# Output projections by seven quarter products: the last branch's additions and the sums of merged quarters on the vector engine, half of the sums ahead of the last branch tiles

## The chip, the core and the metric

The kernel runs on one core of a Trainium2 chip. The core has engines that run their own instruction rows side by side and wait for each other by semaphores. The profile calls them PE (TensorE, matrix products), PEld (its weight loads), DVE (VectorE), ACT (ScalarE), POOL (GpSimd) and SP (SyncE, which issues most of the loads). The metric is the device time of one execution in microseconds (us). Matrix products read their operands from the on-chip memory SBUF and write into banks of a second memory, PSUM; POOL's instructions in this kernel work on SBUF alone.

## What is computed

Two layers of a hybrid encoder on 512 tokens of width 1024. Each layer runs three branches (a pooling mixer, a sparse attention, an attention into memory tokens). What this change touches is the end of a layer, where the branches are projected, weighted by gates, added up and projected once more:

```python
for l in range(DEPTH):
    ...
    g = jax.nn.sigmoid(gates).reshape(b, s, N_BRANCH, D_MODEL)
    merged = (g[:, :, 0] * (y_pool @ w_branch[l, 0])
              + g[:, :, 1] * (y_attn @ w_branch[l, 1])
              + g[:, :, 2] * (y_mem @ w_branch[l, 2]))
    x = x + merged @ w_out[l]
return rms_norm(x, final_g)
```

## The kernel before

**Numbers in two parts.** Every float32 operand of a matrix product is split into a rounded high part and the rest (hi and lo), and a product is three matmuls: hi with hi, hi with lo, lo with hi. For a weight chunk of 128x1024, ACT writes the high part (`whi`, L172) and DVE the low part (`wlo`, L151 or L176, raw minus high). For activations `split_scaled` does the same with a factor: ACT writes the high part (L158), DVE the low part (L159). The normalised input of a layer stands as eight such pairs `h_hi[k]`, `h_lo[k]` (in the profile hh and hl).

**Branch tiles.** The merged sum has 1024 channels, in eight tiles j = 0 to 7 of 128 channels by 512 tokens. For each branch, a gate tile (`gate_tile`, 24 matmuls that read all eight pairs h, then a tanh on ACT) makes the gate `sg`, and a branch tile (`branch_tile`, L764) makes two tiles j from one weight chunk: 12 matmuls each into a PSUM bank, then on DVE gate plus one times bank (L771), then an addition into the tile's accumulator `acc[j]` (L775, on POOL). The branches run in the order 0, 2, 1; branch 1, the attention, is the last. After each pair of its tiles, `merge` (L781) splits the finished accumulators into the pairs `quarter` (in the profile mgh and mgl): for tiles 0 to 3 the first 256 tokens, for tiles 4 to 7 both halves of the tokens.

**Seven quarter products.** The output projection is a product of two matrices cut into quarters (first and second 256 tokens, first and second 512 channels of the sum, first and second 512 columns). Instead of eight quarter products it makes seven, from sums and differences of quarters, in Winograd's way. On the side of the activations these are four sums s1 to s4 (tiles `ms`), made by `quarter_sums(c)` (L790) in two halves: c = 0 needs the accumulators 0, 1, 4 and 5, c = 1 needs 2, 3, 6 and 7. For each c there are eight instructions of 128x256, four on DVE (L796, L797) and four on POOL (L798, L799). `quarter_split(n)` (L801) splits a sum into the pairs h, which no gate tile needs any more once the last one has read them: the sums of c = 0 go into h[0], h[2], h[4], h[6], those of c = 1 into h[1], h[3], h[5], h[7]. On the side of the weights POOL makes four differences of 128x1024 for each half c: b12 minus b11 in the place of b11 (L1000), b22 minus that (L1001, t2), b22 minus b12 in the place of b12 (L1018), b21 minus t2 in the place of b21 (L1014). L1000 overwrites b11, so it waits until DVE has read it for `wlo`; L1014 waits for b21's in the same way.

**The order of the products** (L998 to L1030): quarter by b11 into the banks `at`, quarter by b21 into two `pj` banks (24 matmuls each, first the 12 of c = 0, then the 12 of c = 1), then the second sum by t2 into `at`, the first sum by the new b11 into `tr`, and so on. In layer 0 the residual stream is then normalised for layer 1; in layer 1 the output is scaled and stored.

**What sets the order.** Each engine takes its instructions strictly in the order of its row. The rows come from the order of the code and from a scheduler that may pull an instruction ahead of others on its engine; so the place of an instruction is read from the rows of the built program. Tiles share buffers, and an instruction that writes one waits until the last reader of the tile before is done.

Of the kernel before, what the change touches and what calls it, by code (L numbers as in the profile page):

```python
# [52 lines left out]
def kernel(  # L53
# [19 lines left out]
    V, A, G, T = nc.vector, nc.scalar, nc.gpsimd, nc.tensor  # L73
# [28 lines left out]
    def s2(base, dt=F32, shape=(P, S)):  # L102
        return work.tile(list(shape), dt, tag="s2", name=nm(base), bufs=N_S2)
# [53 lines left out]
    def split_scaled(hi, lo, src, scale):  # L157
        on_act[:] = [A.mul(hi, src, scale)]  # L158
        return V.scalar_tensor_tensor(lo, src, scale, hi.bitcast(F32), op0=ALU.mult, op1=ALU.subtract)  # L159

    def chunk(src, n=1024, eng=None):
        return split_chunk(raw_chunk(src, n), n, eng)
# [27 lines left out]
    def project(c, r_hi, r_lo, nk=KT, off=0, m=P, c0=0, n=S, out=None):  # L190

        hi, lo = c
        ps = pj() if out is None else out
        for k in range(nk):
            a = slice(off + k * m, off + k * m + m)
            mm3(ps[:m, :n], hi[:, a], lo[:, a], r_hi[k][:, c0:c0 + n], r_lo[k][:, c0:c0 + n],
                k == 0, k == nk - 1)
        return ps
# [82 lines left out]
    def product(banks, a_parts, w_parts, start, by_tile=False):  # L281

        def unit(c, t):
            (a_hi, a_lo), (hi, lo) = a_parts[c], w_parts[c]
            for a in range(2):
                w = slice(a * 512, a * 512 + 512)
                tk = slice(a * 256 + t * P, a * 256 + t * P + P)
                for n, (u, v) in enumerate(((a_hi, hi), (a_hi, lo), (a_lo, hi))):
                    matmul(banks[t], u[:, tk], v[:, w], start=start and c == 0 and a == 0 and n == 0,
                           stop=c == 1 and a == 1 and n == 2, skip_group_check=True)  # L290

        order = [(c, t) for t in range(2) for c in range(2)] if by_tile else [(c, t) for c in range(2)
                                                                              for t in range(2)]
        for c, t in order:
            unit(c, t)

    def out_add(x, i, f, banks):

        for t in range(2):
            V.tensor_add(x[2 * i + t][f], x[2 * i + t][f], banks[t])  # L300
# [46 lines left out]
    for i in range(4):  # L347
# [4 lines left out]
        for a in range(2):  # L352
            if i == 0:
                c = slice(a * 512, (a + 1) * 512)
# [8 lines left out]
        for a in range(2):  # L363
            c = slice(a * 512, (a + 1) * 512)
# [42 lines left out]
    for k in range(KT):  # L407
        hi, lo = parts_k[k // 2]
        for h in range(4):
            o = banks[h // 2][:, h % 2 * M:h % 2 * M + M]  # L410
            c = slice(k % 2 * 512 + h * P, k % 2 * 512 + h * P + P)
# [94 lines left out]
    for l in range(DEPTH):  # L506
# [36 lines left out]
        for i in range(4):  # L543
            c = first_iq if l == 0 and i == 0 else chunk(w_tiled[l, TILE_AT["iq"] + i])
# [211 lines left out]
        acc, gate = {}, {}  # L756

        def gate_tile(bi, j):
            ps = tiled(l, f"g{bi}", j)
            s = s2("sg")  # L760
            A.activation(s, ps, AF.Tanh, scale=0.5)
            gate[bi, j] = s

        def branch_tile(bi, jp):  # L764
            b = "pam"[bi]
            c = chunk(w_br[l, bi, jp])
            for a in range(2):
                j = 2 * jp + a
                s = gate.pop((bi, j))
                ps = project(c, [yh[b, i] for i in range(4)], [yl[b, i] for i in range(4)], nk=4, off=a * 512)  # L770
                last = V.scalar_tensor_tensor(s, s, 1.0, ps, op0=ALU.add, op1=ALU.mult)  # L771
                if j not in acc:
                    acc[j] = s
                else:
                    G.tensor_add(acc[j], acc[j], s)  # L775
            return last

        quarter, sums = {}, {}
        first, second = slice(0, 256), slice(256, 512)

        def merge(j):  # L781
            n, c, a = j // 4, j % 4 // 2, j % 2
            for i in range(2 if n else 1):
                if a == 0:
                    quarter[i, n, c] = s2("mgh", F32R), s2("mgl", F32R)
                hi, lo = quarter[i, n, c]
                o = slice(a * 256, a * 256 + 256)
                split_scaled(hi[:, o], lo[:, o], acc[j][:, second if i else first], 0.5)

        def quarter_sums(c):  # L790
            s1, s2_, s3, s4 = (s2("ms") for _ in range(4))
            sums[1, c], sums[2, c], sums[3, c], sums[4, c] = s1, s2_, s3, s4
            for a in range(2):
                k = 2 * c + a
                o = slice(a * 256, a * 256 + 256)
                V.tensor_add(s1[:, o], acc[k][:, second], acc[4 + k][:, second])  # L796
                V.tensor_sub(s2_[:, o], s1[:, o], acc[k][:, first])  # L797
                G.tensor_sub(s3[:, o], acc[k][:, first], acc[k][:, second])  # L798
                G.tensor_sub(s4[:, o], acc[4 + k][:, first], s2_[:, o])  # L799

        def quarter_split(n):  # L801
            out = []
# [6 lines left out]
        def branch_units(bi):  # L809
            out = []  # L810
            for jp in range(4):
                out += [lambda j=2 * jp + a: gate_tile(bi, j) for a in range(2)]
                out.append(lambda jp=jp: branch_tile(bi, jp))
            return out
# [148 lines left out]
        for jp in range(4):  # L963
            for a in range(2):
                gate_tile(1, 2 * jp + a)
            branch_tile(1, jp)
            for a in range(2):
                merge(2 * jp + a)


        src = x_tok if l == 0 else x1
# [31 lines left out]
        w = w_split(b21)  # L1003
        out_add(x, 0, 0, at)
        product(pw2, [quarter[0, 1, c] for c in range(2)], w, True)
        for c in range(2):
            quarter_sums(c)
        out_add(x, 0, 0, pw2)
        out_done(l, x, 0, 0, ssq, grow if last else None)
        a_parts, w = quarter_split(2), w_split(t2)  # L1010
# [127 lines left out]
```

## Time and profile before

| | before |
|---|---|
| median of 3 runs | 1074.49 us (1073.6 to 1074.76) |
| the profiled execution, its own time | 1073.67 us |
| its span, first to last instruction | 1071.9 us |
| mean granted clock of TensorE | 0.984 of full speed |
| chain of work that ended last, by engine | PE 89%, POOL 4%, DVE 3%, issue, ACT and DMA 1% each |
| output projection of layer 0 begins | 483.4 us |
| output projection of layer 1 begins | 1010.65 us |

A row of a timeline gives the start in us from the span's start, the duration in us, the engine, the line of the kernel, the operation, the tiles it writes and reads, the shapes, how many equal instructions it stands for (x2: two, one behind the other), and in brackets the idle time just before and what ended it. A row of the waits gives who waited for whom, the sum in us, how many times, and the longest. The profile gives a start as the time at which the engine takes up an instruction; where it is held up by something other than a semaphore, that time is part of its duration.

### The profile page before, as it was taken

Reading aid. Unit: us, or ns where it says so; the run is one execution under the profiler, and the core shown is the slowest. Engines: PE = TensorE matmul, PEld = TensorE weight load, DVE = VectorE, ACT = ScalarE, POOL = GpSimd, SP = SyncE. Lnnn points to the kernel's source line nnn. Section 1 sums busy time; section 2 is a strip of 40 time slices with the busy share of each in tenths; the row PEclk is TensorE's granted clock in tenths of the full one; section 3 lists DMA queues with packets and bytes.
Section 4 is the critical chain, followed back from the end, with each engine's and each line's share of the span. In section 5 each row is a group of like instructions: output and inputs, shape, how many; then the busy total and the mean of one; then the engine's idle time right before and its main releaser. Section 6 shows DMA issues by size and latency. Waiting matters only on the chain.

```text
span 1071.9 us, 13685 instructions
## 1 busy us (share of the span) xinstructions
PE 1045.2 (98%) x4982; PEld 876.8 (82%) x4982; DVE 751.1 (70%) x1338; ACT 494.5 (46%) x900; POOL 264.3 (25%) x322
## 2 busy tenths in 40 slices
PE   9999999999999999996999999999999999999967
PEld 9888888888888888884898888888888888888845
DVE  7768878777888746355854687887768886543496
ACT  7755554322656434333564555542235554333254
POOL 3102420011242310257050042100113431011851
PEclk9999999999999999997999999999999999999969
DMA  9322234232323234230454121222332223322302
GB/s 344 127 91 89 80 111 145 79 122 102 111 72 108 97 118 156 97 121 1 169 177 133 64 105 63 79 79 94 114 108 99 98 79 106 132 97 99 118 0 79
DMA packets 37411, 114.24 MB, mean 107 GB/s; under 512 B 4184, under 2 KB 6232, under 8 KB 37344
## 3 DMA queue, kind: packets, MB, share of 16 engines
q1 hardware_dynamic: 35472, 110.20, 29.9%
q10 hardware_dynamic: 1872, 3.17, 0.8%
q8 instruction: 39, 0.64, 0.2%
q14 instruction: 28, 0.23, 0.1%
HBM read 109.14 MB, written 6.84 MB: 108 GB/s over the span
## 4 chain that ended last, share of the span: by engine, by line
PE 89%; POOL 4%; DVE 3%; issue 1%; ACT 1%; DMA 1%; SPq 0%; POOLq 0%; ACTq 0%; DVEq 0%
PE pj L86 67%; PE at L86 11%; PE pv L86 5%; PE tr L86 3%; PE tr L634 2%; POOL wraw L1000 1%; POOL wraw L1018 1%; POOL sg L775 1%; DVE mgl L159 1%; DMA x<-x 0%; POOL ow L1001 0%; DVE ms L797 0%; DVE ms L796 0%; POOL ow L1014 0%; DVE wlo L176 0%
## 5 line engine op out<-in xcount | busy, mean ns | idle before, releaser
L172 ACT CAST whi<-wraw 128x1024 fp32r<-128x1024 f32 x168 | 175.5, 1046 | 336.3 <-PE pj L86 192.5
L86 PE MATMUL pj<-hh,whi 128*128 128x512 f32 (+1 forms) x848 | 330.6, 390 | 0.0
L86 PE MATMUL pj<-hl,whi 128*128 128x512 f32 (+1 forms) x848 | 328.9, 388 | 0.0
L86 PE MATMUL pj<-hh,wlo 128*128 128x512 f32 (+1 forms) x848 | 328.8, 388 | 0.0
L151 DVE TENSOR_TENSOR wlo<-wraw,whi 128x1024 fp32r<-128x1024 f32 x140 | 179.2, 1281 | 126.8 <-ACT whi L172 126.3
L86 PEld LDWEIGHTS pj<-hh,wlo 128*128 128x128 f32 x848 | 159.3, 188 | 32.0
L86 PEld LDWEIGHTS pj<-hh,whi 128*128 128x128 f32 x848 | 159.4, 188 | 30.5
L86 PEld LDWEIGHTS pj<-hl,whi 128*128 128x128 f32 x848 | 159.4, 188 | 30.4
L775 POOL TENSOR_TENSOR sg<-sg,sg 128x512 f32<-128x512 f32 x32 | 52.3, 1636 | 230.2 <-DVE sg L771 228.2
L86 PE MATMUL pj<-yh,whi 128*128 128x512 f32 x192 | 75.2, 392 | 0.0
L86 PE MATMUL pj<-yl,whi 128*128 128x512 f32 x192 | 74.8, 390 | 0.0
L86 PE MATMUL pj<-yh,wlo 128*128 128x512 f32 x192 | 74.8, 390 | 0.0
L845 POOL TENSOR_TENSOR p<-rel,mask 128x128 f32<-128x128 f32 x16 | 7.5, 466 | 254.2 <-DMA rel<-bias_row 251.0
L845 POOL TENSOR_TENSOR p<-rel,acc 128x256 f32<-128x256 f32 (+2 forms) x48 | 61.1, 1294 | 0.5
L771 DVE SCALAR_TENSOR_TENSOR sg<-sg,pj 128x512 f32<-128x512 f32 x48 | 32.9, 685 | 35.6 <-PE pj L86 35.5
L159 DVE SCALAR_TENSOR_TENSOR mgl<-sg,mgh 128x256 fp32r<-128x256 f32 x24 | 21.8, 936 | 44.6 <-ACT mgh L158 44.6
L607 DVE MATCH_REPLACE8 acc<-m,acc 128x256 f32<-128x256 f32 (+2 forms) x96 | 51.4, 542 | 0.0
L861 DVE CUSTOM_DVE_ANT_0 p<-at,p 128x128 f32<-128x128 f32 (+1 forms) x64 | 30.0, 490 | 27.3 <-PE at L86 26.9
L606 DVE MAX8 m<-acc 128x8 f32<-128x256 f32 (+2 forms) x96 | 49.0, 548 | 0.1
L86 PEld LDWEIGHTS pj<-yh,wlo 128*128 128x128 f32 x192 | 36.1, 188 | 7.5
L86 PEld LDWEIGHTS pj<-yl,whi 128*128 128x128 f32 x192 | 36.1, 188 | 7.2
L86 PEld LDWEIGHTS pj<-yh,whi 128*128 128x128 f32 x192 | 36.1, 188 | 7.2
(258 smaller groups left out, 1867.5 us busy)
## 6 DMA issues: line engine op xcount, KB each, us to landing
wraw<-in_w_tiled SPq DMA_DIRECT2D x112, 512.0 KB, 3.3
wraw<-in_w_br SPq DMA_DIRECT2D x24, 512.0 KB, 3.5
wraw<-in_w_mv SPq DMA_DIRECT2D x8, 512.0 KB, 5.3
wraw<-in_w_av SPq DMA_DIRECT2D x8, 512.0 KB, 3.5
rel<-bias_row SPq DMA_DIRECT2D x16, 256.0 KB, 3.7
ow<-in_w_out SPq DMA_DIRECT2D x8, 512.0 KB, 3.5
wraw<-in_w_out SPq DMA_DIRECT2D x8, 512.0 KB, 3.5
wraw<-in_w_mk SPq DMA_DIRECT2D x7, 512.0 KB, 4.5
```

What stands on the lines that cost most here:

```text
L86: on_pe[:] = [T.matmul(*a, **kw)]
L151: eng.tensor_sub(out_lo, src, hi)
L159: return V.scalar_tensor_tensor(lo, src, scale, hi.bitcast(F32), op0=ALU.mult, op1=ALU.subtract)
L172: A.copy(hi[:, :n], raw[:, :n])
L606: V.max(m8, a[:, :n])
L607: V.match_replace(out=a[:, :n], in_to_replace=m8, in_values=a[:, :n], imm_value=TAKEN)
L634: T.transpose(pt[:, i * P:(i + 1) * P], col_of(qb, kb), ident)
L771: last = V.scalar_tensor_tensor(s, s, 1.0, ps, op0=ALU.add, op1=ALU.mult)
L775: G.tensor_add(acc[j], acc[j], s)
L845: G.tensor_add(probs[h][:, Q_COL[qb]:Q_COL[qb] + n], rels[h][:, 512 - n:512], mb[:, :n])
L861: V.tensor_tensor_reduce(out=pq, in0=ps[:, :n], in1=pq, op0=ALU.add, op1=ALU.min, scale=-1.0, scalar=3e38, accum_out=st[:, 0, qb:qb + 1])
L1000: G.tensor_sub(b11[c], b12[c], b11[c])
```

## The change

Three edits, in both layers:

- the additions of the last branch (branch 1) into the accumulators, eight for each layer, run on DVE; those of branch 2 stay on POOL;
- the sums s3 and s4, which were on POOL, run on DVE with s1 and s2;
- the first half of the sums (c = 0) is made behind the third pair of branch tiles (tiles 4 and 5), ahead of the last pair; the second half (c = 1) behind the last pair. Before, both stood in the code behind the second product.

```diff
@@ branch_tile
                 if j not in acc:
                     acc[j] = s
                 else:
-                    G.tensor_add(acc[j], acc[j], s)
+                    (V if bi == 1 else G).tensor_add(acc[j], acc[j], s)
@@ quarter_sums
                 V.tensor_add(s1[:, o], acc[k][:, second], acc[4 + k][:, second])
                 V.tensor_sub(s2_[:, o], s1[:, o], acc[k][:, first])
-                G.tensor_sub(s3[:, o], acc[k][:, first], acc[k][:, second])
-                G.tensor_sub(s4[:, o], acc[4 + k][:, first], s2_[:, o])
+                V.tensor_sub(s3[:, o], acc[k][:, first], acc[k][:, second])
+                V.tensor_sub(s4[:, o], acc[4 + k][:, first], s2_[:, o])
@@ the loop over the last branch's tiles
             branch_tile(1, jp)
             for a in range(2):
                 merge(2 * jp + a)
+            if jp > 1:
+                quarter_sums(jp - 2)
@@ behind the second product
         product(pw2, [quarter[0, 1, c] for c in range(2)], w, True)
-        for c in range(2):
-            quarter_sums(c)
         out_add(x, 0, 0, pw2)
```

(In the code of the change L1000 and L1001 have become L1002 and L1003; the other lines that are named here keep their numbers.)

What that makes of the rows is seen in three places, all in layer 0; in layer 1 the rows there are in the same order.

**DVE, from b11's first low part to the merge of tile 6.** sg_4414 and sg_4426 are the gates of tile 6 before and in the change; the `wlo` from `wraw` are the two halves of b11, the `wlo` from `ow` the first half of b21. Before, from the L771 of tile 5:

```order
L771 SCALAR_TENSOR_TENSOR sg_4333<-sg_4333,pj_4356 128x512
L176 TENSOR_TENSOR wlo_4539<-wraw_4514,whi_4538 128x1024
L159 SCALAR_TENSOR_TENSOR mgl_4372<-sg_2393,mgh_4371 128x256
L159 SCALAR_TENSOR_TENSOR mgl_4376<-sg_2393,mgh_4375 128x256
L176 TENSOR_TENSOR wlo_4543<-wraw_4516,whi_4542 128x1024
L176 TENSOR_TENSOR wlo_4575<-ow_4518,whi_4574 128x1024
L771 SCALAR_TENSOR_TENSOR sg_4414<-sg_4414,pj_4455 128x512
L159 SCALAR_TENSOR_TENSOR mgl_4486<-sg_2487,mgh_4485 128x256
```

In the change, from b11's first low part:

```order
L176 TENSOR_TENSOR wlo_4563<-wraw_4538,whi_4562 128x1024
L799 TENSOR_TENSOR ms_4386<-sg_2393,ms_4384 128x256
L176 TENSOR_TENSOR wlo_4567<-wraw_4540,whi_4566 128x1024
L159 SCALAR_TENSOR_TENSOR hl_159<-ms_4383,hh_151 128x512
L159 SCALAR_TENSOR_TENSOR hl_161<-ms_4384,hh_153 128x512
L159 SCALAR_TENSOR_TENSOR hl_163<-ms_4385,hh_155 128x512
L159 SCALAR_TENSOR_TENSOR hl_165<-ms_4386,hh_157 128x512
L176 TENSOR_TENSOR wlo_4599<-ow_4542,whi_4598 128x1024
L771 SCALAR_TENSOR_TENSOR sg_4426<-sg_4426,pj_4467 128x512
L775 TENSOR_TENSOR sg_2487<-sg_2487,sg_4426 128x512
L159 SCALAR_TENSOR_TENSOR mgl_4498<-sg_2487,mgh_4497 128x256
```

The low parts of four sums (hl of h[0], h[2], h[4], h[6]) now stand ahead of b21's low part and of tile 6's L771; the two low parts of b11 stand behind the merge of tile 5 and seven of the eight sums of c = 0, where before the first of them stood ahead of that merge.

**DVE, from the L771 of tile 7 to the addition of the first product to x.** sg_4447 and sg_4459 are the gates of tile 7; wlo_4579 and wlo_4603 are the low part of b21's second half. Before:

```order
L771 SCALAR_TENSOR_TENSOR sg_4447<-sg_4447,pj_4470 128x512
L176 TENSOR_TENSOR wlo_4579<-ow_4520,whi_4578 128x1024
L159 SCALAR_TENSOR_TENSOR mgl_4486<-sg_2520,mgh_4485 128x256
L159 SCALAR_TENSOR_TENSOR mgl_4490<-sg_2520,mgh_4489 128x256
L176 TENSOR_TENSOR wlo_4645<-ow_4530,whi_4644 128x1024
L300 TENSOR_TENSOR x_4497<-x_4497,at_4532 128x512
```

In the change:

```order
L771 SCALAR_TENSOR_TENSOR sg_4459<-sg_4459,pj_4482 128x512
L797 TENSOR_TENSOR ms_4510<-ms_4509,sg_2229 128x256
L775 TENSOR_TENSOR sg_2520<-sg_2520,sg_4459 128x512
L798 TENSOR_TENSOR ms_4511<-sg_2229 128x256
L799 TENSOR_TENSOR ms_4512<-sg_2487,ms_4510 128x256
L159 SCALAR_TENSOR_TENSOR mgl_4498<-sg_2520,mgh_4497 128x256
L159 SCALAR_TENSOR_TENSOR mgl_4502<-sg_2520,mgh_4501 128x256
L796 TENSOR_TENSOR ms_4509<-sg_2262,sg_2520 128x256
L798 TENSOR_TENSOR ms_4511<-sg_2262 128x256
L797 TENSOR_TENSOR ms_4510<-ms_4509,sg_2262 128x256
L176 TENSOR_TENSOR wlo_4603<-ow_4544,whi_4602 128x1024
L799 TENSOR_TENSOR ms_4512<-sg_2487,ms_4510 128x256
```

The low part of b21's second half stood directly behind the L771 of tile 7; now the merge of tile 7 and six sums of c = 1 stand between.

**POOL, at the weight differences.** Before (the L775 are the additions of tiles 4 to 7):

```order
L775 TENSOR_TENSOR sg_2360<-sg_2360,sg_4300 128x512
L775 TENSOR_TENSOR sg_2393<-sg_2393,sg_4333 128x512
L1000 TENSOR_TENSOR wraw_4514<-wraw_4522,wraw_4514 128x1024
L1001 TENSOR_TENSOR ow_4530<-ow_4526,wraw_4514 128x1024
L1018 TENSOR_TENSOR wraw_4522<-ow_4526,wraw_4522 128x1024
L1000 TENSOR_TENSOR wraw_4516<-wraw_4524,wraw_4516 128x1024
L1001 TENSOR_TENSOR ow_4531<-ow_4528,wraw_4516 128x1024
L1018 TENSOR_TENSOR wraw_4524<-ow_4528,wraw_4524 128x1024
L1014 TENSOR_TENSOR ow_4518<-ow_4518,ow_4530 128x1024
L775 TENSOR_TENSOR sg_2487<-sg_2487,sg_4414 128x512
L775 TENSOR_TENSOR sg_2520<-sg_2520,sg_4447 128x512
L1014 TENSOR_TENSOR ow_4520<-ow_4520,ow_4531 128x1024
```

In the change:

```order
L1002 TENSOR_TENSOR wraw_4538<-wraw_4546,wraw_4538 128x1024
L1003 TENSOR_TENSOR ow_4554<-ow_4550,wraw_4538 128x1024
L1018 TENSOR_TENSOR wraw_4546<-ow_4550,wraw_4546 128x1024
L1002 TENSOR_TENSOR wraw_4540<-wraw_4548,wraw_4540 128x1024
L1003 TENSOR_TENSOR ow_4555<-ow_4552,wraw_4540 128x1024
L1018 TENSOR_TENSOR wraw_4548<-ow_4552,wraw_4548 128x1024
L1014 TENSOR_TENSOR ow_4542<-ow_4542,ow_4554 128x1024
L1014 TENSOR_TENSOR ow_4544<-ow_4544,ow_4555 128x1024
```

The eight differences are now all that POOL has here. Each L1002 waits for the low part of its half of b11 on DVE, each L1014 for that of its half of b21.

On ACT the high parts of the four early sums (L158, hh of h[0], h[2], h[4], h[6]) stand ahead of the cast of b21's first half and of the last gate's tanh. The loads of the residual stream x (eight on SP) use other buffers than before, and seven of them wait for DVE's additions, sums or merges of tiles 4 and 5, or for the first of those hl.

## Prediction

> **What bounds the kernel now.** I read the page first, then the granted clock in stretches, the waits of the bad stretch, and last the timelines of the four engines there.
>
> ```profile
> PE 1045.2 (98%) x4982; PEld 876.8 (82%) x4982; DVE 751.1 (70%) x1338; ACT 494.5 (46%) x900; POOL 264.3 (25%) x322
> 455.00:491.50 36.50, 36.50 (x163) 30.08 (x161) 15.59 (x13) 8.92 (x15) 22.42 (x10) 1.00 0.27 95
> 491.50:511.20 19.70, 11.03 (x24) 6.50 (x24) 17.98 (x23) 10.59 (x19) 11.63 (x10) 0.65 0.03 11
> 511.20:530.00 18.80, 18.80 (x84) 15.54 (x83) 16.73 (x21) 9.68 (x13) 0.23 (x2) 1.00 0.46 158
> 1018.80:1040.20 21.40, 12.35 (x27) 7.67 (x27) 19.72 (x24) 10.52 (x19) 14.50 (x12) 0.60 0.00 0
> ```
>
> The columns of a stretch are its length, busy time of PE, PEld, DVE, ACT and POOL, the clock, and DMA. TensorE is the bound except in one stretch of each layer, at the start of the output projection: there PE works 11 of 19.7 us, at clock 0.65. What that costs is counted from one row of the chain of waits, where PE runs unhindered, and from PE's timeline:
>
> ```profile
> 170.87 97.71 PE pj L86 x431
> ...
> 491.34 0.39 PE L86 MATMUL pj<-whi,mgl 128*128 128x512 f32 x1
> 511.14 0.39 PE L86 MATMUL at<-wlo,hh 128*128 128x512 f32 x1
> ...
> 1018.59 0.39 PE L86 MATMUL pj<-whi,mgl 128*128 128x512 f32 x1
> 1040.23 0.39 PE L86 MATMUL at<-whi,hh 128*128 128x512 f32 x1
> ```
>
> At full clock matmuls start every 0.227 us (431 in 97.71). Layer 0: the row of 511.14 is 23 matmuls behind the first, 5.2 us, but comes 19.8 us later: 14.6 us lost. Layer 1: 27 matmuls, 6.1 us, and 21.6 us: 15.5 lost. Together 30 us; the change cannot bring more here. What PE waits for:
>
> ```profile
> ACT mgh L158 <- POOL sg L775: 14.1, 2, 11.7
> DVE mgl L159 <- ACT mgh L158: 11.6, 2, 10.0
> ACT hh L158 <- DVE ms L796: 5.2, 2, 4.4
> POOL ms L799 <- DVE ms L797: 3.4, 1, 3.4
> PE at L86 <- ACT hh L158: 2.9, 1, 2.9
> PE at L86 <- DVE hl L159: 2.6, 1, 2.6
> ```
>
> The last two merges wait for POOL's addition, and the sums come late behind them. Why POOL is late:
>
> ```profile
> 470.77 2.39 POOL L1000 TENSOR_TENSOR wraw<-wraw,wraw 128x1024 f32<-128x1024 f32 x1
> ...
> 475.66 2.57 POOL L1018 TENSOR_TENSOR wraw<-ow,wraw 128x1024 f32<-128x1024 f32 x1
> 479.39 3.31 POOL L1000 TENSOR_TENSOR wraw<-wraw,wraw 128x1024 f32<-128x1024 f32 x1 [1.16 <-DVE wlo L176]
> 482.78 2.39 POOL L1001 TENSOR_TENSOR ow<-ow,wraw 128x1024 f32<-128x1024 f32 x1
> 485.13 2.40 POOL L1018 TENSOR_TENSOR wraw<-ow,wraw 128x1024 f32<-128x1024 f32 x1
> 487.48 2.40 POOL L1014 TENSOR_TENSOR ow<-ow,ow 128x1024 f32<-128x1024 f32 x1
> 489.84 1.29 POOL L775 TENSOR_TENSOR sg<-sg,sg 128x512 f32<-128x512 f32 x1
> 493.04 2.19 POOL L775 TENSOR_TENSOR sg<-sg,sg 128x512 f32<-128x512 f32 x1 [1.92 <-DVE sg L771]
> ```
>
> Tile 6 was ready for its addition at 481.6 (the L771 below), but POOL had four weight subtractions of 2.4 us ahead of it. That queue goes with the change. The question is what takes its place.
>
> **How DVE and POOL meet.** DVE's rows in the same place:
>
> ```profile
> 468.44 1.22 DVE L176 TENSOR_TENSOR wlo<-wraw,whi 128x1024 fp32r<-128x1024 f32 x1
> L159 DVE SCALAR_TENSOR_TENSOR mgl<-sg,mgh x2: 2153/2381/2609, 471.3 to 473.4; 128x256 fp32r<-128x256 f32 x2
> 475.90 3.41 DVE L176 TENSOR_TENSOR wlo<-wraw,whi 128x1024 fp32r<-128x1024 f32 x1
> 479.24 1.21 DVE L176 TENSOR_TENSOR wlo<-ow,whi 128x1024 fp32r<-128x1024 f32 x1
> 480.88 0.69 DVE L771 SCALAR_TENSOR_TENSOR sg<-sg,pj 128x512 f32<-128x512 f32 x1 [0.44 <-PE pj L86]
> 491.61 0.76 DVE L159 SCALAR_TENSOR_TENSOR mgl<-sg,mgh 128x256 fp32r<-128x256 f32 x2 [10.04 <-ACT mgh L158]
> 502.83 1.82 DVE L796 TENSOR_TENSOR ms<-sg,sg 128x256 f32<-128x256 f32 x2
> 504.58 1.81 DVE L797 TENSOR_TENSOR ms<-ms,sg 128x256 f32<-128x256 f32 x2
> ```
>
> Two mgl take 0.76 us alone, but 2.15 and 2.61 us each beside POOL's subtractions. The wlo of 475.90 ends at 479.31, 1.1 us after the L1018 ended at 478.23; the L1000 of 479.39 ends 2.3 us after the wlo of 479.24 did. L771, whose second input is in PSUM, is not touched (0.69 beside that L1000). So a DVE instruction with two SBUF inputs and a POOL one run one after the other, and where both have work they take turns, one each: at 502.8 four sums of 0.33 us take 3.6 us beside four of POOL's. One turn is 2.3 us for a POOL subtraction; for DVE 1.13 (128x1024), 0.6 (128x512), 0.33 (128x256), from rows that follow each other.
>
> **The change part by part.** Durations are of the profiled execution: 1073.67 us, a span of 1071.9 and 1.8 around it; the median of the runs is 1074.49, 0.8 more.
>
> Additions of tiles 0 to 5 onto DVE: six of 128x512 for each layer. Their form is not in DVE's rows; the nearest are L771 (0.69) and hl (0.69 at 519.65), the contended end is 0.6 plus one turn. I take 0.6. For the first four nothing of POOL's runs beside them and DVE waits for its next cast anyway, so they cost nothing; without that cover 0.6 each.
>
> ```profile
> 462.70 1.22 DVE L151 TENSOR_TENSOR wlo<-wraw,whi 128x1024 fp32r<-128x1024 f32 x1 [4.21 <-ACT whi L172]
> 464.56 0.69 DVE L771 SCALAR_TENSOR_TENSOR sg<-sg,pj 128x512 f32<-128x512 f32 x1 [0.64 <-PE pj L86]
> ...
> 519.65 0.69 DVE L159 SCALAR_TENSOR_TENSOR hl<-ms,hh 128x512 fp32r<-128x512 f32 x1
> L796 DVE TENSOR_TENSOR ms<-sg,sg x8: 410/678/950, 501.5 to 1032.1; 128x256 f32<-128x256 f32 x8
> ```
>
> Tiles 4 and 5 with the first four sums, layer 0, from the L771 of 464.56: two L771 and two additions (2.5 with the wait between the first pair), a wait of 0.48 for ACT's mgh (as from POOL's end at 491.13 to the mgl of 491.61), four mgl (1.35), seven of the eight sums (0.33 each, 410 ns with its end: 2.3), and the wlo of the first weight half of b11 (1.13): it ends near 472.4, where before it ended at 469.66. It releases POOL's first subtraction, so POOL begins 2 us later than now (470.77), at 472.8 behind the eighth sum.
>
> From there POOL has six subtractions in a row with nothing between (no addition stops it now), and DVE has six pieces: wlo of b11's second half, the four hl that the early sums allow, and wlo of b21's first half. Taking turns they are plainly added: 6 x 2.3 + 1.13 + 4 x 0.6 + 1.13 = 18.5 us, so that wlo lands at 491.3, where before it was there at 480.45. PE wants it with the second matmul of its product, at 489.1 (the row of 491.34 is the product's twelfth): **a new wait of 2.2 us**. The product's second bank waits for the L771 of tile 6, which comes 0.6 later and is hidden behind its first six matmuls. ACT's four hh ahead of its casts cost nothing: it sat idle 3.9 us at 477.9 for the same last gate tile (the row is below).
>
> The L771 of tile 6, due at 480.88, stands behind that wlo: 491.9. Beside it POOL takes its seventh piece, L1014, to 493.7; then the addition (0.6), the wait for mgh and two mgl (1.2), four sums, L771 and addition of tile 7, two mgl and three more sums (4.2 us in all), and wlo of b21's second half (1.13): 500.9. POOL's eighth piece waits for that wlo, so it is idle meanwhile. PE wants it at 491.8, with the fourteenth matmul. **PE is then 9.1 us late in all**, the 2.2 included. Its clock is down again and comes back as now:
>
> ```profile
> 507.57 0.79 PE L86 MATMUL at<-whi,hl 128*128 128x512 f32 x1 [2.59 <-DVE hl L159]
> 510.73 0.58 PE L86 MATMUL at<-whi,hh 128*128 128x512 f32 x1
> ...
> 477.94 1.05 ACT L172 CAST whi<-ow 128x1024 fp32r<-128x1024 f32 x1 [3.90 <-PE pj L86]
> ```
>
> For 3.5 us from the restart at 507.57 matmuls start every 0.43 us (the row of 510.73 is the seventh behind it, and the first took 0.6); that is 8 of them, 1.6 us more than at full clock. So the stretch loses 10.8 us instead of 14.6 in layer 0, and instead of 15.5 in layer 1, whose rows of DVE and POOL are the same up to here. The late sums (L796 to L799 behind both products, 5 us on the chain now) are gone from the chain: the second four lie in the 500.9. What is late next is wlo of t2, at 505.4 and 506.5 behind two additions to x, POOL's last subtraction and one hl; PE asks for the first about 505.2 and the second at 507.9, so at most 0.2 us. The loads of x, which now wait for DVE's sums in SP's queue, are issued by 480, the last behind the first hl, and read at 501: free.
>
> Sum: 3.8 + 4.7 = **8.4 us off**, 1073.67 to 1065.3; on the scale of the median 1066.1. I say 1066.0. If the clock needs as long again to come back, each layer loses 1.5 more (1069); a POOL turn of 2.25 or 2.35 moves it by 0.7.
>
> **The rivals.** *DVE is not held up*: all of the 30 us come back, 1044. For it: DVE is idle 10 us at 491.61 now. Against it: 2.15 and 2.61 us for a piece of 0.33. The Trainium skill, SBUF — State Buffer, section Who interferes with whom, says that of a VectorE instruction with two SBUF inputs and a GpSimd one that reads SBUF the second to issue blocks until the first is done; by that rule this rival falls, and the trace agrees (2.61 us).
>
> *DVE goes first whenever it is ready*: POOL gets only DVE's gaps, five turns ahead of the last wlo instead of seven (4.6 us), and DVE's waits for mgh (1.2) lie beside them: 5.8 us sooner; but the remaining subtractions then fall on the hl and wlo of the next product and give back some 3.5. A net 2.3 for each layer: 1061. For it: wlo at 479.24 started ahead of L1000. Against it: that one waited for the wlo before it; after mgl, L1018 went first.
>
> *Slower: a turn costs the contended duration.* If each of the seven POOL turns takes the 3.31 us of the L1000 row and not 2.3, wlo of b21's second half comes 7.1 us later: 1065.3 + 14.1 = 1079. It decides from 0.6 us for each turn, where both gains are used up. Against it: that 3.31 holds 1.0 us of waiting for DVE, which I count on DVE's side. The Trainium skill, Perfetto Trace Analysis, section Optimizing Scalar/DVE Operations, says of GPSIMD and DVE that offloading between those two might not help, because they share a read port; by that rule the sum would be near nothing, 1074, between my forecast and this rival.
>
> *The change does its work but the new row of DVE eats it*: the 0.6 us a turn just named, 1072 to 1076.
>
> **How the numbers follow.** Turns as counted 0.71 (1062 to 1069); DVE first 0.12; not held up 0.06; used up 0.05; slower 0.06. The range 1059 to 1070 holds the first and most of the second. A measurement of this kernel can tell 0.2%, 2.1 us, from no change: faster 0.89, same 0.05, slower 0.06.
>
> **What would show it.** On PE in layer 0: a wait of about 2 us for wlo near 489, a long one for wlo near 492 to 501, none for POOL's addition and none for hh; clock below 0.8 in that stretch, 11 us lost. On DVE: the four hl from 478 to 488, each about 2.9 us, in turn with POOL; L771 of tile 6 near 491. PE without a gap from 483 to 530 would show the first rival, POOL rows of 3.3 us one after the other with a restart behind 504 the third.

## The result, and the profile after

The kernel with the change takes 1065.15 us (median of 4 runs, 1064.73 to 1066.0) beside 1074.05 us for the one before (4 runs on the same chip, 1073.39 to 1074.76): a ratio of 0.9918, with a 95% interval of 0.9901 to 0.9935. The execution that was profiled took 1064.73 us, with a span of 1062.9; before it was 1073.67 and 1071.9.

The page's first part:

```profile
PE 1038.3 (98%) x4982; PEld 873.3 (82%) x4982; DVE 773.1 (73%) x1370; ACT 494.5 (47%) x900; POOL 226.3 (21%) x290
```

Two stretches, one of each layer (length, busy time of PE, PEld, DVE, ACT and POOL, clock, DMA):

```profile
488.90:507.50 18.60, 10.90 (x39) 8.09 (x40) 18.08 (x27) 8.55 (x15) 5.03 (x3) 0.82 0.04 15
1010.00:1034.00 24.00, 16.22 (x57) 12.13 (x56) 23.48 (x28) 10.78 (x19) 10.24 (x5) 0.79 0.00 0
```

POOL is busy 38 us less and DVE 22 us more. TensorE still has one bad stretch in each layer, and beside it DVE is now busy nearly all the time (18.08 of 18.60 us), where before it was 18.0 of 19.7. What the stretch costs now, from PE's timeline (the rows of 504.72 and 1028.77 are the 27th matmul behind the first one of their layer):

```profile
488.24 0.39 PE L86 MATMUL pj<-whi,mgh 128*128 128x512 f32 x1
490.26 0.50 PE L86 MATMUL pj<-wlo,mgh 128*128 128x512 f32 x1 [1.63 <-DVE wlo L176]
...
494.99 0.50 PE L86 MATMUL pj<-whi,mgh 128*128 128x512 f32 x1 [1.93 <-ACT whi L172]
499.89 0.80 PE L86 MATMUL pj<-wlo,mgh 128*128 128x512 f32 x1 [4.41 <-DVE wlo L176]
...
502.62 0.44 PE L86 MATMUL pj<-wlo,mgh 128*128 128x512 f32 x1
...
504.72 0.40 PE L86 MATMUL at<-whi,hh 128*128 128x512 f32 x1
1011.25 0.39 PE L86 MATMUL pj<-whi,mgh 128*128 128x512 f32 x1
...
1022.94 0.79 PE L86 MATMUL pj<-wlo,mgh 128*128 128x512 f32 x1 [4.17 <-DVE wlo L176]
...
1028.23 0.47 PE L86 MATMUL at<-wlo,hh 128*128 128x512 f32 x1
...
1028.77 0.40 PE L86 MATMUL at<-whi,hh 128*128 128x512 f32 x1
```

And what PE waits for in the whole execution (us in total, times, longest):

```profile
PE pj L86 <- DVE wlo L176: 11.9, 4, 4.4
PE pj L86 <- ACT whi L172: 3.9, 2, 1.9
```

27 matmuls at full pace are 6.1 us. Layer 0: 504.72 less 488.24 is 16.5, so 10.4 us are lost. Layer 1: 17.5, so 11.4 lost. Together 21.7 where it was 30.1: 8.4 us of the 8.9 between the two profiled executions. The rest lies ahead of the stretch: the L771 of tile 4 starts at 463.96 here and at 464.56 before. In the other kernels below it starts anywhere from 463.91 (sums_only) to 465.68 (late_sums_weights), so nothing is read into it, nor into differences of about 1 us between the start times of two kernels.

DVE's timeline of layer 0 there:

```profile
463.96 0.69 DVE L771 SCALAR_TENSOR_TENSOR sg<-sg,pj 128x512 f32<-128x512 f32 x1 [0.59 <-PE pj L86]
473.03 2.63 DVE L176 TENSOR_TENSOR wlo<-wraw,whi 128x1024 fp32r<-128x1024 f32 x1 [0.72 <-ACT whi L172]
475.58 11.30 DVE L159 SCALAR_TENSOR_TENSOR hl<-ms,hh 128x512 fp32r<-128x512 f32 x4
486.81 3.40 DVE L176 TENSOR_TENSOR wlo<-ow,whi 128x1024 fp32r<-128x1024 f32 x1
490.13 0.68 DVE L771 SCALAR_TENSOR_TENSOR sg<-sg,pj 128x512 f32<-128x512 f32 x1
490.84 2.40 DVE L775 TENSOR_TENSOR sg<-sg,sg 128x512 f32<-128x512 f32 x1
498.62 1.22 DVE L176 TENSOR_TENSOR wlo<-ow,whi 128x1024 fp32r<-128x1024 f32 x1
```

And POOL's:

```profile
472.11 2.47 POOL L1002 TENSOR_TENSOR wraw<-wraw,wraw 128x1024 f32<-128x1024 f32 x1 [75.74 <-DMA x<-in_x_tok]
474.65 3.27 POOL L1003 TENSOR_TENSOR ow<-ow,wraw 128x1024 f32<-128x1024 f32 x1
477.87 2.86 POOL L1018 TENSOR_TENSOR wraw<-ow,wraw 128x1024 f32<-128x1024 f32 x1
480.69 2.84 POOL L1002 TENSOR_TENSOR wraw<-wraw,wraw 128x1024 f32<-128x1024 f32 x1
```

These rows show the turns. Four hl of 0.6 us take 11.3, because between each two of them one of POOL's subtractions runs, (11.3 - 4 x 0.6) / 4 = 2.2 us a turn; the wlo behind them takes 3.4 where it takes 1.22 alone. That wlo ends at 490.2, PE wanted it at 488.5.

### The profile page after: what moved, and what is told of

Its sections match the earlier page's. It is cut to its first block, busy times and chain, and to the rows that moved or that the text cites. A ratio compares the mean times of both kernels' runs of the same rounds, so it can differ in the third digit from the quotient of the medians.

```text
span 1062.9 us, 13690 instructions
## 1 busy us (share of the span) xinstructions
PE 1038.3 (98%) x4982; PEld 873.3 (82%) x4982; DVE 773.1 (73%) x1370; ACT 494.5 (47%) x900; POOL 226.3 (21%) x290
## 4 chain that ended last, share of the span: by engine, by line
PE 93%; DVE 5%; ACT 1%; issue 1%; POOL 0%; POOLq 0%; ACTq 0%
PE pj L86 71%; PE at L86 10%; PE pv L86 5%; PE tr L86 3%; PE tr L634 2%; DVE hl L159 2%; DVE wlo L176 1%; DVE sg L775 1%; ACT whi L172 0%; PE tr L324 0%; DVE mgl L159 0%; PE at L324 0%; DVE sg L771 0%; DVE o L333 0%; DVE ms L797 0%
## 5 line engine op out<-in xcount | busy, mean ns | idle before, releaser
L771 DVE SCALAR_TENSOR_TENSOR sg<-sg,pj 128x512 f32<-128x512 f32 x48 | 32.9, 684 | 36.0 <-PE pj L86 36.0
L775 POOL TENSOR_TENSOR sg<-sg,sg 128x512 f32<-128x512 f32 x16 | 24.6, 1536 | 100.3 <-DVE sg L771 100.3
L1002 POOL TENSOR_TENSOR wraw<-wraw,wraw 128x1024 f32<-128x1024 f32 x4 | 10.6, 2655 | 151.5 <-DMA x<-x 75.8
```

The lines of the kernel that those rows point to most:

```text
L775: (V if bi == 1 else G).tensor_add(acc[j], acc[j], s)
```

## The experiments

The theory: with the additions gone from POOL, its weight subtractions meet DVE's row directly, and the 21.7 us still lost are POOL's turns. The rivals: the early sums are what pays; DVE's own row is full; each meeting costs a fixed extra. The same numbers for all runs, each beside the kernel before on the same chip ("lost" is summed from PE's timeline of the profiled execution: each start to start in the stretch less 0.227 us). In before_weights the profiled execution took 1058.36 us, 3.2 more than the median; in the others it lies within 1.3 of it.

```
kernel               median us   ratio to before, 95%     lost, layers 0 and 1
the change           1065.15     0.9918 [0.9901, 0.9935]  10.4  11.4
adds_only            1067.38     0.9934 [0.9920, 0.9947]  11.2  12.1
late_sums            1066.79     0.9925 [0.9913, 0.9938]  10.6  12.3
sums_only            1070.17     0.9964 [0.9951, 0.9976]  13.3  13.2
weights_dve          1045.42     0.9730 [0.9717, 0.9743]  0.0   0.5
before_weights       1055.16     0.9828 [0.9815, 0.9842]  8.4   6.0
late_sums_weights    1052.07     0.9790 [0.9772, 0.9807]  2.3   5.0
pool_halves          1062.49     0.9893 [0.9879, 0.9906]  9.8   9.7
hl_held              1060.89     0.9879 [0.9865, 0.9892]  7.9   9.4
early_diffs_dve      1060.01     0.9869 [0.9856, 0.9883]  6.9   8.2
late_diffs_dve       1060.10     0.9859 [0.9840, 0.9878]  6.5   9.0
```

### The parts of the change

**adds_only**: in the change, the sums as before.

```diff
-            if jp > 1:
-                quarter_sums(jp - 2)
...
+        for c in range(2):
+            quarter_sums(c)
...
-                V.tensor_sub(s3[:, o], acc[k][:, first], acc[k][:, second])
-                V.tensor_sub(s4[:, o], acc[4 + k][:, first], s2_[:, o])
+                G.tensor_sub(s3[:, o], acc[k][:, first], acc[k][:, second])
+                G.tensor_sub(s4[:, o], acc[4 + k][:, first], s2_[:, o])
```

> Only the first edit: the last branch's additions on DVE, all sums back at their old place (half of them on POOL). Theory (turns, one each, 2.3 us for each POOL subtraction): POOL's run of subtractions starts about 471 and nothing of POOL's stands before tile 6 any more; without the four early hl fewer DVE pieces stand in the turns, so wlo of b21 lands before PE wants it, but the late sums are back behind both products, beside POOL. Counted as in the prediction, 11.6 and 12.5 us lost in the two layers against 10.9 each with the whole change: 1067, so three quarters of the gain (1074 to 1067) come from the additions alone. Rival (the sums made early are what pays): the late sums cost as before, 4 to 5 us a layer of the old loss, and this kernel stands at 1070 to 1073.

**late_sums**: the first two pieces of that diff alone, so all sums on DVE, at their old place.

> Additions and all sums on DVE, but none of the sums early. Theory: DVE does the eight sums in 0.33 us each instead of taking turns with POOL's four, some 0.3 to 1 us less for each layer than with the additions alone: 1066.5, that is, within a measurement of the whole change (1065.2): the early place of half the sums is worth at most 1 to 2 us, because it takes four hl into the turns ahead of wlo. Rival (early sums pay): 1069 or more.

**sums_only**:

```diff
-                    (V if bi == 1 else G).tensor_add(acc[j], acc[j], s)
+                    G.tensor_add(acc[j], acc[j], s)
```

> Sums as in the change, the last branch's additions on POOL as before. Theory: tiles 6 and 7 are added on POOL behind seven subtractions and hl in turns: 13.5 us lost for each layer, 1070, so the sums alone bring less than half. Rival (the additions are not what matters): within 1 us of the whole change, 1065 to 1066.

Measured: 1067.4, 1066.8 and 1070.2, each within 0.4 us of what the turns gave. PE's waits in adds_only:

```profile
PE at L86 <- ACT hh L158: 11.4, 2, 6.1
PE pj L86 <- DVE wlo L176: 0.4, 2, 0.2
```

In sums_only, one of PE's waits and one of ACT's (that one of the stretch of layer 0):

```profile
PE pj L86 <- ACT whi L172: 12.0, 2, 6.0
ACT mgh L158 <- POOL sg L775: 24.0, 4, 16.5
```

Without the early sums PE gets wlo in time and waits for the hh of the late sums instead; with the additions on POOL it waits behind POOL's addition (6.0 us for whi, whose cast stands behind mgh, and then 4.9 for wlo). So the additions bring the larger part. What the early half adds to that, 1.6 us by the medians and 0.8 by the ratios (0.9925 and 0.9918), lies inside the intervals: it takes the late sums off the chain and puts four hl, with a turn each, ahead of wlo.

### POOL's weight differences

**weights_dve**: the change, and L1002, L1003, L1014 and L1018 on DVE.

```diff
-            G.tensor_sub(b11[c], b12[c], b11[c])
-            G.tensor_sub(t2[c], b22[c], b11[c])
+            V.tensor_sub(b11[c], b12[c], b11[c])
+            V.tensor_sub(t2[c], b22[c], b11[c])
...
-            G.tensor_sub(b21[c], b21[c], t2[c])
+            V.tensor_sub(b21[c], b21[c], t2[c])
...
-            G.tensor_sub(b12[c], b22[c], b12[c])
+            V.tensor_sub(b12[c], b22[c], b12[c])
```

> The change, and the eight weight differences of each layer on DVE as well, so that POOL does nothing in the stretch. Theory (POOL's turns are what makes wlo late): a difference takes 1.13 us on DVE and nobody waits for a turn; wlo of b21's halves land near 480 and 490, before PE wants them (488.5 and 491), and nearly all of the 22 us still lost come back: 1043 to 1046. Rival (DVE's own row is full, the turns are not the price): 9 us more work on DVE for each layer in the same stretch, wlo later by up to that: 1070 to 1083. Rival in between (some other wait, such as the second bank or x, takes over): 1050 to 1060, with that wait named on PE.

Measured: 1045.42, inside the first of these ranges. The stretch of layer 0:

```profile
488.90:507.50 18.60, 18.60 (x83) 15.39 (x82) 18.55 (x25) 10.44 (x15) 0.00 (x0) 1.00 0.34 112
```

DVE's timeline there:

```profile
472.90 1.22 DVE L1002 TENSOR_TENSOR wraw<-wraw,wraw 128x1024 f32<-128x1024 f32 x1
474.04 1.22 DVE L176 TENSOR_TENSOR wlo<-wraw,whi 128x1024 fp32r<-128x1024 f32 x1
479.18 1.22 DVE L176 TENSOR_TENSOR wlo<-ow,whi 128x1024 fp32r<-128x1024 f32 x1
489.28 1.22 DVE L176 TENSOR_TENSOR wlo<-ow,whi 128x1024 fp32r<-128x1024 f32 x1
```

PE runs through this stretch, at full clock; in layer 1 it loses 0.5 us. DVE has 18 us more of its own work in the two layers than in the change and is done with the last wlo 9 us sooner: a difference takes 1.14 us there (472.90 to 474.04), where it took 2.3 on POOL and held DVE up for as long. So the rival of DVE's full row falls: the row has more in it and ends sooner. This kernel beats both, the one before and the change.

**before_weights**: the same four lines (L1000, L1001, L1014, L1018) in the kernel before, nothing of the change.

> The kernel before, nothing of the change, with the eight weight differences of each layer on DVE. Theory: the four subtractions ahead of POOL's addition (9.8 us) are gone, so tile 6 is added at 482; what is left is the late sums behind both products and the clock, 6 to 7 us for each layer: 1056 to 1059. Rival (the additions on POOL are the trouble, wherever the differences run): 1066 or more. Rival (the weights were all of it): 1045, as with the change.

**late_sums_weights**: weights_dve with the sums behind both products, as in late_sums.

> Additions, all sums and all eight weight differences on DVE, but none of the sums early (they stay behind both products). Theory: with POOL out of the way the place of the sums is what is left: sixteen sums of 0.33 us, hh and hl stand on the chain behind tile 7 and the additions to x, 3.9 and 5 us lost in the two layers: 1053 to 1056, so that the early half, worth 1.6 us while POOL took its turns, is worth some 9 us once POOL is out. Rival (the early half brings nothing of its own): 1045 to 1047, as with the sums early.

Measured: 1055.16 and 1052.07, 0.8 and 0.9 us below the bounds given: the late sums were priced a little too high (3.9 us in layer 0 of late_sums_weights, where 2.3 were lost). PE's waits in before_weights:

```profile
PE at L86 <- ACT hh L158: 5.2, 2, 3.0
PE at L86 <- DVE hl L159: 2.8, 1, 2.8
```

In late_sums_weights:

```profile
PE at L86 <- DVE hl L159: 5.1, 2, 3.1
```

Moving each layer's eight weight differences, with nothing of the change, brings 18.8 us (1073.95 beside it), twice what the change brings; and what the change brings beyond that is some 10 (0.9828 to 0.9730). The early half of the sums, not measurable while POOL took its turns, is worth 6 to 7 us once POOL is out (0.9790 to 0.9730).

### Size, place and number of the turns

**pool_halves**: each of POOL's differences as two pieces.

```diff
-            G.tensor_sub(b11[c], b12[c], b11[c])
+            for a in (slice(0, 512), slice(512, 1024)):
+                G.tensor_sub(b11[c][:, a], b12[c][:, a], b11[c][:, a])
```

(and the other three lines in the same way)

> The change with each of POOL's weight differences cut into two pieces of 128x512: the same work on POOL, turns half as long, twice as many. Theory (turns, one each; what counts is POOL's whole work ahead of the last wlo): six DVE pieces now meet six halves of 1.2 us, so wlo of b21's first half lands near 484.5 instead of 490.2 and PE's first wait (1.6 us) is gone; but the other eight halves then stand between the additions, mgl and sums, and wlo of b21's second half lands within 2 us of the 499.8 of now: 9 to 11 us lost for each layer, 1063 to 1066, no gain to speak of. Rival (each meeting costs a fixed extra, the third rival of the prediction): twice the meetings, 0.5 us or more for each of 14: 1072 to 1080. Rival (a DVE piece waits only for the piece of POOL that is running, and nothing is added up): the last wlo comes 5 us or more sooner, 1055 or below.

Measured: 1062.49. DVE's timeline of layer 0:

```profile
475.08 6.89 DVE L159 SCALAR_TENSOR_TENSOR hl<-ms,hh 128x512 fp32r<-128x512 f32 x4
481.89 2.31 DVE L176 TENSOR_TENSOR wlo<-ow,whi 128x1024 fp32r<-128x1024 f32 x1
497.73 1.21 DVE L176 TENSOR_TENSOR wlo<-ow,whi 128x1024 fp32r<-128x1024 f32 x1
```

PE's waits:

```profile
PE pj L86 <- DVE wlo L176: 14.1, 2, 7.1
```

Each hl now waits (6.89 - 4 x 0.6) / 4 = 1.1 us, half as long, and wlo of b21's first half ends at 484.2, 6 us sooner; the last wlo ends at 498.9, only 0.9 sooner. The first wait is gone and the second one longer, as expected, with 9.8 and 9.7 us lost. The time is 0.5 us below the bound given. Twice the meetings cost nothing, so the third rival of the prediction falls.

**hl_held**: the hl of L159 behind the last wlo of b21 in DVE's row (issue_after sets that order on their engine).

```diff
-            eng.tensor_sub(lo[:, :n], raw[:, :n], hi[:, :n])
+            on_dve[:] = [eng.tensor_sub(lo[:, :n], raw[:, :n], hi[:, :n])]
...
-                split_scaled(h_hi[k], h_lo[k], sums[n, c], 0.5)
+                with tc.issue_after(hold.ins):
+                    split_scaled(h_hi[k], h_lo[k], sums[n, c], 0.5)
...
         w = w_split(b21)
+        hold = on_dve[0]
```

> The change with the hl of the early sums kept behind wlo of b21's second half in DVE's row. Theory: four DVE pieces of 0.6 us and the four turns of POOL's that they let in no longer stand ahead of wlo of b21's first half, which lands by 482; L771 of tile 6 follows there, and the POOL turns left are met by the addition, mgl and sums instead; counted over, 8 to 8.7 us lost for each layer instead of 10.9: 1059 to 1061. Rival (the hl are not in the way, POOL's total is all that counts): 1064 to 1066. Rival (hl later costs as much behind): 1065 or more, with a wait of PE for hl.

Measured: 1060.89, inside. PE's waits:

```profile
PE pj L86 <- DVE wlo L176: 11.0, 2, 5.6
```

One wait for wlo is left in each layer. So 4 us of the 20 that weights_dve brings come back by order alone; the others stay with POOL's turns, met by other DVE pieces (in layer 0 two mgl, 0.76 us alone, take 4.6).

**early_diffs_dve** and **late_diffs_dve**: of the diff of weights_dve the lines of L1002 and L1003 alone, or those of L1014 and L1018 alone.

> The change with four of the eight differences of each layer on DVE (those of L1002 and L1003), the other four left on POOL. Theory: four turns of POOL's fewer ahead of wlo of b21, three or four left: 5 to 6 us lost for each layer instead of 10.9 and of nothing with all eight moved: 1053 to 1057, about half way, as the price goes by the number of POOL's turns. Rival (only the first ones matter, or only the last): 1045 to 1047, or 1062 to 1065.

> The change with the other four differences of each layer on DVE (L1014 and L1018) and those of L1002 and L1003 left on POOL. Theory: four POOL turns left, now at the start of the stretch, where POOL comes in first and every DVE piece behind it is held up (in the run with the other four on POOL, POOL's first subtraction was kept out for 4.9 us by five DVE pieces in a row, so who is first matters): 8 to 9 us lost for each layer: 1060 to 1063. Rival (the price goes by the number of turns alone, wherever they fall): 1053 to 1057.

Measured: 1060.0 and 1060.1. The first expectation missed by 3 us. The second holds by its median, at its lower end, but the five runs of late_diffs_dve fall apart (1056.1 and 1056.6, and 1060.1 to 1060.8, at mean granted clocks of 0.994 and of 0.990 to 0.991), and layer 0 lost 6.5 us where 8 to 9 were expected, so its rival (1053 to 1057) is not clearly out. Half of the differences bring 5 or 6 us, all of them 20.

The first expectation had counted turns and left out that each difference that moves costs DVE 1.14 us of its own. Net of that a turn of 2.2 saved is worth 1.1: some 4 us for four of them in each layer, and 3.5 and 3.2 came back in early_diffs_dve (10.4 to 6.9, 11.4 to 8.2). That all eight bring the last wlo 9.3 us sooner in layer 0 (499.8 to 490.5), and with it the clock's share, is seen. With half of them moved another wait takes over. In early_diffs_dve the last wlo of b21 ends at 492.8, 7 us sooner than in the change, and then PE waits for mgl and for the additions to x:

```profile
PE at L86 <- DVE x L300: 5.9, 2, 3.5
PE pj L86 <- DVE mgl L159: 3.1, 2, 1.6
```

DVE reaches those additions (L300) at 500.28 in layer 0, no sooner than in the change (500.09), for it has met POOL's four subtractions that are left on the way (8.8 us) and done the four moved ones; with all eight moved it reaches them at 490.75. So half a move shortens the way to wlo, but not DVE's row behind it. Whether that is all of the difference was not tested.

One thing that the turns had not foreseen is in the rows: POOL's first subtraction was kept out (early_diffs_dve; POOL's instructions that touch wraw in layers 0 and 1, with the shortest, median and longest in ns, and the first and last start):

```profile
L1018 POOL TENSOR_TENSOR wraw<-ow,wraw x2: 3377/5324/7272, 474.2 to 481.4; 128x1024 f32<-128x1024 f32 x2
L1018 POOL TENSOR_TENSOR wraw<-ow,wraw x2: 2840/6228/9617, 993.8 to 1003.4; 128x1024 f32<-128x1024 f32 x2
```

DVE's timeline there, of layer 0 and, in the last two rows, of layer 1:

```profile
474.00 1.22 DVE L176 TENSOR_TENSOR wlo<-wraw,whi 128x1024 fp32r<-128x1024 f32 x1
475.13 1.22 DVE L1003 TENSOR_TENSOR ow<-ow,wraw 128x1024 f32<-128x1024 f32 x1
476.27 1.22 DVE L1002 TENSOR_TENSOR wraw<-wraw,wraw 128x1024 f32<-128x1024 f32 x1
477.40 0.68 DVE L159 SCALAR_TENSOR_TENSOR hl<-ms,hh 128x512 fp32r<-128x512 f32 x1
478.01 1.22 DVE L1003 TENSOR_TENSOR ow<-ow,wraw 128x1024 f32<-128x1024 f32 x1
479.14 3.42 DVE L176 TENSOR_TENSOR wlo<-ow,whi 128x1024 fp32r<-128x1024 f32 x1
...
1001.10 0.68 DVE L771 SCALAR_TENSOR_TENSOR sg<-sg,pj 128x512 f32<-128x512 f32 x1
1001.70 2.30 DVE L159 SCALAR_TENSOR_TENSOR hl<-ms,hh 128x512 fp32r<-128x512 f32 x1
```

The L1018 issued at 474.2 lasts 7.3 us, 9.6 in layer 1: DVE runs five pieces one behind the other without giving it a turn, and only the sixth is held up. That sixth reads a cast of ACT's that ended at 479.10, 0.04 us before; whether this let POOL in is not shown (in layer 1 the same cast ended 0.09 us before, and POOL stayed out). In layer 1 eight pieces go ahead, and the one held up is the hl behind an L771, whose second input is in PSUM. In the change DVE had waited 0.72 us for ACT's cast (the row of 473.03), POOL came in there, and from then on the turns were one each.

**gap_op**: early_diffs_dve, and a small DVE instruction amid those five; its result is not used.

```diff
             V.tensor_sub(t2[c], b22[c], b11[c])
+            V.tensor_scalar(small_tile("gap", [P, 4], bufs=2), t2[c][:, :4], 1.0, None, op0=ALU.mult)
```

> The kernel with the differences of L1002 and L1003 on DVE and the other four on POOL, and one more small DVE instruction (128x4, one SBUF input, its result not used) behind the second L1002, in the middle of the five pieces that kept POOL's first L1018 out for 4.9 us in layer 0 and about 7 in layer 1. Theory (DVE keeps the common access as long as its next instruction with two SBUF inputs follows without a gap; any instruction that does not need it lets POOL in): POOL's L1018 gets in at that instruction in both layers, near 477.4 in layer 0, and lasts 5.6 us in both instead of 7.3 and 9.6; the hl behind the small one, 0.68 us so far, takes some 2.9. Rival (the small instruction does not let POOL in; POOL gets in only where DVE waits or reads PSUM): L1018 lasts 7.3 and more as before, and that hl 0.68.

Measured in a single execution: 1058.0. POOL's instructions on wraw in layer 0 (L1019 is the L1018 of the others):

```profile
L1019 POOL TENSOR_TENSOR wraw<-ow,wraw x2: 5188/5370/5551, 474.1 to 479.6; 128x1024 f32<-128x1024 f32 x2
```

DVE's timeline:

```profile
477.28 2.38 DVE L1004 TENSOR_SCALAR gap<-ow 128x4 f32<-128x4 f32 x1
479.58 0.68 DVE L159 SCALAR_TENSOR_TENSOR hl<-ms,hh 128x512 fp32r<-128x512 f32 x1
480.19 1.21 DVE L1003 TENSOR_TENSOR ow<-ow,wraw 128x1024 f32<-128x1024 f32 x1
481.32 1.21 DVE L176 TENSOR_TENSOR wlo<-ow,whi 128x1024 fp32r<-128x1024 f32 x1
```

POOL comes in at the small instruction, and its L1018 lasts 5.55 us in both layers, as the theory had it. But the small instruction itself is held up for the 2.3 us, not the hl behind it; and behind it three more pieces run in a row while POOL's second subtraction, issued at 479.6, waits. It comes in at the next small instruction (482.46, held up in the same way, 2.36 us). So here an instruction of another kind in DVE's row decided when POOL got in, in both layers. What else counts as such a break, and why the small instruction waits too, is left open.

## Why the prediction was right, point by point

- **What bounds the kernel.** PE, with one bad stretch in each layer: weights_dve, whose stretch has PE busy all the time, takes 29 us less than the kernel before on the same chip (1045.42 beside 1074.47), of the 30 that the prediction set as the most.
- **The turns.** 2.3 us for each of POOL's was the term; the four hl show 2.2. They ran from 475.6 to 486.9, where the prediction had said 478 to 488; its own sum (472.8 and a turn of 2.3 and 1.13) begins them at 476.2. The Trainium skill, SBUF — State Buffer, section Who interferes with whom, says that issue order decides which of the two blocks. The trace agrees where POOL was first in the change, but not in early_diffs_dve: POOL's L1018 was issued at 474.2, ahead of four more DVE pieces that still went before it, and took 7.3 us in all.
- **The two waits for wlo.** Forecast 2.2 us at 489.1, with wlo at 491.3; measured 1.8 (490.26 less 488.24 and one matmul), wlo at 490.2. Forecast 9.1 in all with the last wlo at 500.9; measured 8.7 (499.89 less 488.24 and 13 matmuls), at 499.8. Wlo came 1.1 sooner: 0.7 because POOL began sooner (472.11 beside 472.8) and the rest by slightly shorter turns; PE itself was 0.6 sooner, so its wait is 0.4 shorter.
- **A wait that was not named.** The thirteenth matmul waited for whi (1.93 us): ACT's cast of b21's second half stands behind mgh of tile 6, and that behind the addition. It costs nothing, as wlo of the same half is later still.
- **The clock.** 1.6 us for each layer were taken. Of the matmuls behind the last wait, those of layer 0 keep the 0.43 us pace for 2.7 us (499.89 to 502.62) and lose 1.4, those of layer 1 for 5.3 (1022.94 to 1028.23) and lose 2.6. The prediction had that as a bound: 1.5 more for a layer whose clock needs as long again. The stretch was to run at a clock below 0.8; it was 0.82 in layer 0 and 0.79 in layer 1.
- **The sum.** 10.8 for each layer against 10.4 and 11.4: 21.6 to 21.7, and 8.4 off to 8.4 measured. 1066.0 against 1065.15. That the sums agree to 0.1 is luck: wlo cost 0.4 less than forecast in each layer, and the clock 0.2 less in one and 1.0 more in the other. The terms of the prediction, 9.1 and 1.6, add up to 10.7 and not 10.8, and 3.8 and 4.7 to 8.5; this moves the forecast by 0.1 or 0.2.
- **What was free.** PE waits neither for POOL's addition nor hh nor x. Wlo of t2 was to cost at most 0.2 us; the two matmuls from 503.82 to 504.49 take 0.67 for 0.45.
- **The rivals.** "Not held up" falls by 2.2 us a turn, and its 1044 is what comes out when POOL's work is really taken away (1045.42). "DVE first" has a point, in the rows of early_diffs_dve, but not where DVE has to wait for ACT first, as it does in the change. "Slower" falls by the turns of 2.2 us, and a fixed extra for each meeting by pool_halves. "The new row of DVE eats it" needed 0.6 us more for each turn; the turns were 0.1 shorter. The Trainium skill, Perfetto Trace Analysis, section Optimizing Scalar/DVE Operations, says that offloading between GPSIMD and DVE might not help, because of the shared read port: the trace agrees for GPSIMD's work beside DVE's (a turn of 2.2 us for each piece), and not for the way back (1045.42), since the same subtraction takes DVE half the time.

## What to carry to other kernels

Where VectorE's instructions with two SBUF inputs and GpSimd's meet in one stretch, as here, add their rows up as if they were one engine's, and charge GpSimd's work at its longer duration. A subtraction of 128x1024 took 2.3 us on GpSimd and 1.14 on VectorE, so moving all of them to VectorE shortened VectorE's own row. Moving half of them brought much less than half. A move that takes an instruction out of a slow queue is worth little while the queue itself stays in the way; look first at what the queue does. A part that measures as nothing may be covered by another bound: the early sums were worth at most 1.6 us, inside the error, and 6 to 7 once POOL was out.

## What the runs showed of the hardware that was not expected

VectorE and GpSimd do not always alternate. In early_diffs_dve a row of VectorE's two-input instructions without a gap, begun before GpSimd's subtraction was issued, kept that one waiting for 4.9 us in layer 0 (five pieces) and over 7 in layer 1. Once a two-input instruction of VectorE's had itself been held up, the two took turns, there as in the change; behind the small instruction of gap_op they did not. GpSimd got in where VectorE waited for ACT (0.72 us in the change), behind an L771 with its PSUM input, or at the small instruction of gap_op; these are the cases seen, and no rule was tested beyond gap_op. And the clock came back after 2.7 us in one layer and 5.3 in the other, behind nearly the same waits (1.63, 1.93 and 4.41 us, and 1.68, 1.93 and 4.17).
